# An encoder layer on one core: earlier first weights, and another order of loads at the weight switches and before the tail

## The chip, the cores and the metric

The kernel runs on one core of a Trainium2 chip. The metric is the time of one execution on the device in microseconds (us). The five engines that the profile names are PE (TensorE, matrix products), DVE (VectorE), ACT (ScalarE), POOL (GpSimd) and SP (SyncE, which here issues every DMA). Each engine works through its own instructions in order and waits where a semaphore tells it to.

## The reference

One layer of a bidirectional encoder is applied to two groups of 2048 tokens with a model width of 1024:

```python
h = rms_norm(x)
q_a, k_a, v_a, g_a, q_b, k_b, v_b, g_b = split(h @ w_in)      # 512,128,128,512, 512,512,512,512
o_a = windowed_gqa_sink(rope(norm(q_a)), rope(norm(k_a)), v_a) * silu(g_a)   # 8 heads, 2 kv heads, +-128 tokens
o_b = neighbourhood_attn(norm(q_b), norm(k_b), v_b, rpb) * silu(g_b)         # 8 heads, 8 x 16 window on a 64-wide grid
x = x + concat(o_a, o_b) @ w_out
return x + (p @ w_ple) * sigmoid(x @ w_ple_gate)
```

Branch A is a windowed attention with a sink, branch B a neighbourhood attention on a grid with a learned relative position bias. All is float32.

## The kernel before

**Precision.** Each float32 operand of a product is split into a high part and a low remainder, and a product is three matrix products. For weights `split_w` does it: ScalarE writes the high part (L147 with the norm's scale, L151 without), VectorE the low part (L148, L152). For a token tile `split` does it: ScalarE the high part (L294), GpSimd the low part (L295).

**Tiles.** Tokens go in tiles of 128, 16 per group, 32 in all. A running number f counts the work: f = 0 to 31 is branch A (`proj_a`, `unit_a`), f = 32 to 63 the first half of branch B's heads, f = 64 to 95 the second half (`proj_b`, `unit_b`). Then `out_ahead(0)` to `out_ahead(3)` compute the output projection (`pout`) of four blocks of 256 tokens each, in four products that are numbered mp 0 to 3. The rest of the output projection and the gate of the last line of the reference run in the tail, in a pool of their own ("c"), as products of seven on sums of blocks (`acca`, `accc`, operands `opd`, sums of weights `s1` to `s4`).

**Order.** The projections are generators, chained in `stream`. The attention units draw from the stream between their own steps, so that TensorE has projection work while a softmax runs. A unit of branch B follows its projection by six tiles: unit 57 runs beside the projection of tile 63, unit 89 beside that of tile 95. TensorE's instructions are pinned in program order (`pinned`). The other engines' are ordered by a scheduler from the program's order and its own estimates, save those that `P` (`tc.keep_in_program_order`) pins.

**The first two tiles** are projected together (`first`): `pk` (keys and values of branch A, weights `wx`), then `pq` (queries, weights `w_q`, tag "wa"), then `pg` (gates, `w_g`, tag "wb"). `load_first` stages two blocks of 128 rows of weights at a time in a buffer with the tag "p_t", of which there are three, and splits them at once. The keys and queries go through a normalisation on VectorE (a reciprocal root by iterations, L126 to L133; `kt` L413; `q` L454), a rotation on GpSimd (L426 to L429 for the keys), and a transpose on TensorE (`pkt`, `pqt`), which stands between the products of `pg`. PSUM comes from three pools: "pj" (three banks), "sc" (three) and "ms" (two). `pk`, `pq`, `pg` and `pout` take "pj"; the scores of the attention take "sc".

**Weight switches.** `paired` takes the last two tiles of each stage together (tiles 30 and 31, 62 and 63, 94 and 95), so that the first weight set ("wa") is free while both still use the second ("wb"). `load_w` issues eight loads of 256 KB and puts their splits in the list `jobs`, from which `pump` and `flush` take them while the next products run. "wa" is loaded after both tiles' first product (`pqk`), "wb" after the second tile is finished. At the same time SP issues what the units and tiles need: the tiles' inputs (`stx`, L277), the bias of a unit of branch B (L701), the values with their windows (`vw`, L705, read from `v_d`, where L662 stores `vb`), the unit's output (`ob_d`, L759), and weight rows for the sums (`raw`, L491). A bias has 288, 360, 384 or 512 columns for each of four heads; those of 512 are 1 MB, one for unit 57 and one for unit 89. The softmax (L217, VectorE) adds the bias to the scores (`scb`) in PSUM.

**Passage to the tail.** The sums `s2`, `s1`, `s3` are loaded first (twelve loads of 256 KB, L943), then the last block's inputs, then the raw inputs of the first tail group (`oar` L970 and `obr` L971, 1 MB each), then the residual's blocks. `out_ahead(3)` computes four `pout`. For each it loads a residual block `ev` (L835), adds it on VectorE (L836), which frees the PSUM bank, and stores it (L837). `prep(0)` and `prep(1)` make the first operands of the tail out of `oar` and `obr` (L1000, L1003).

Of the kernel before, what the change touches and what calls it, by code (L numbers as in the profile page):

```python
# [11 lines left out]
F32 = mybir.dt.float32  # L12
# [77 lines left out]
def emit(ctx, tc, io):  # L90
# [79 lines left out]

    def load_w(pool, tag, src, c0, nk, scaled):

        ws = []
        hold[0] = HOLD[tag[:2]]
        for j in range(nk):
            w = pool.tile([128, 2, 512], F32R, tag=f"{tag}{j}", name=f"{tag}{j}", bufs=1)
            raw = w[:, 1].bitcast(F32)
            nc.sync.dma_start(raw, src[128 * j:128 * j + 128, c0:c0 + 512])
            jobs.append((f"{tag}{j}", partial(split_w, w, raw, nw[:, j:j + 1] if scaled else None, P)))
            ws.append(w)  # L180
        return ws

    def load_first(j0, w, src):

        n = w[0].shape[-1]
        st = main.tile([128, 2, 512], F32, tag="p_t", name="ws", bufs=3)
        nc.sync.dma_start(st[:, :, :n], src.rearrange("(j p) c -> p j c", p=128))
        for i in range(2):
            split_w(w[i], st[:, i, :n], nw[:, j0 + i:j0 + i + 1])
# [79 lines left out]
    def load_block(key, tag, bufs):  # L269
        kind, f, i = key  # L270
        staged[key] = main.tile([128, 512], F32, tag=tag, name="st" + kind, bufs=bufs)
        if kind == "n":
            s, t = divmod(f, NT)
            src = io["x_n"][s][128 * t:128 * t + 128]
        else:
            src = io["x_a"][f] if f < 2 * NT else io["x_b"][f % (2 * NT)]
        nc.sync.dma_start(staged[key], src[:, 512 * i:512 * i + 512])  # L277
# [8 lines left out]
    def split(f, i, pin=lambda ins: ins):  # L286
# [30 lines left out]
    def big(shape, dt, name):  # L317
# [15 lines left out]
    for j in range(0, KT // 2, 2):  # L333
        load_first(j, w_q[j:j + 2], io["w_in"][128 * j:128 * j + 256, 256:768])
    for i in range(2):
        load_block(("n", 0, i), "s", SB)
# [24 lines left out]
    nc.sync.dma_start(mask, io["band"])  # L361
    ks_a = big([128, 2, SEQ], F32R, "ks_a")
# [28 lines left out]
    def proj_a(f):  # L391
# [4 lines left out]
        pk = ptile([128, 256], "pj", "pk")  # L396
# [130 lines left out]
    qrest = {}  # L527
# [83 lines left out]
    def proj_b(f):  # L611
# [47 lines left out]
        for w, (c0, ncol) in COL_WIN.items():  # L659
            lo, hi = max(c0, 16 * cb), min(c0 + ncol, 16 * cb + 16)  # L660
            if lo < hi:
                nc.sync.dma_start(v_d[half, s, w][8 * b:8 * b + 8, lo - c0:hi - c0].rearrange("r c h a d -> c r (h a d)"),  # L662
                                  v[8 * (lo - 16 * cb):8 * (hi - 16 * cb)].bitcast(F32).rearrange("p h a d -> p (h a d)"))
# [24 lines left out]
    def unit_b(f):  # L688
# [7 lines left out]
        if cb != 2:  # L696
            off, _ = BIAS_OFF[(row_type(b), col_type(cb))]
            if not bt:
                bt.append(big([128, 2, 4, 512], F32, "bias"))
            bt.append(bt[0][:, len(bt) % 2])  # L700
            nc.sync.dma_start(bt[-1][:, :, :n], io["bias"][half][:, off:off + 4 * n].rearrange("p (h n) -> p h n", h=4))  # L701
        bias = bt[-1]
        vw = [ap.tile([128, 4, 2 * HD], F32R, tag=("vp", "vr_")[j % 2], name="vw", bufs=3 - j % 2) for j in range(nch)]
        for j in range(nch):
            nc.sync.dma_start(vw[j][:kc].bitcast(F32).rearrange("p h d -> p (h d)"),  # L705
                              v_d[half, s, cb][r0 + rows * j:r0 + rows * j + rows]
                              .rearrange("r c h a d -> (r c) (h a d)"))
# [40 lines left out]
        def fin(_):  # L748
# [10 lines left out]
            nc.sync.dma_start(ob_d[s][b, :, 2 * half:2 * half + 2, cb, :], o_t)  # L759
# [17 lines left out]
    def load_o(n, tail):  # L777
        if n < len(tiles):
            s, u = tiles[n]
            o_st[n] = []  # L780
            for i in range(2):
                st = main.tile([128, 2, TW], F32, tag="stage", name="oa", bufs=2)
                nc.sync.dma_start(st, oa_d[s].rearrange("(i j p) t -> i p j t", p=128, j=2)[i, :, :, TW * u:TW * u + TW])
                o_st[n].append(st)
            for i in range(2):
# [4 lines left out]
                nc.sync.dma_start(st.rearrange("p j c t -> p (j c) t"),  # L790
# [25 lines left out]
    def out_ahead(n):  # L816
# [7 lines left out]
        for mp in range(4):  # L824
# [6 lines left out]
            if tail:  # L831
                ev = ap.tile([128, 2, TW], F32, tag="ev", name="ev", bufs=2)
            else:
                ev = main.tile([128, 2, TW], F32, tag="s", name="ev", bufs=SB)
            nc.sync.dma_start(ev, io["x_r"][n][:, 2 * mp:2 * mp + 2])  # L835
            nc.vector.tensor_tensor(out=ev, in0=ps, in1=ev, op=ALU.add)  # L836
# [34 lines left out]
    def paired(f, n):  # L871
# [53 lines left out]
    with tc.tile_pool(name="c", bufs=1) as op:  # L925
# [190 lines left out]
        prep(1)  # L1116
        ws[0]["s4"] = load_q(0, "s4")
# [106 lines left out]
```

## Time and profile before

| | before |
|---|---|
| median of 3 runs | 2605.88 us (2604.47 to 2607.68) |
| the profiled execution | 2603.58 us |
| span of its trace | 2601.7 us |
| mean granted TensorE clock | 0.994 |
| TensorE busy | 2547.1 us, 98% of the span |
| VectorE / ScalarE / GpSimd busy | 1963.3 / 1416.3 / 789.2 us |
| DMA | 357.51 MB, mean 137 GB/s |

The span is the time from the first to the last instruction on the core; the execution's own time is a little longer. In rows of the timeline a time is the start in us from the start of the span, the next number is the length, "x24" counts instructions that stand together, and a bracket gives the idle time before and what ended it. "out<-in" names the tiles that an instruction writes and reads. A row with SPq is the issue of a DMA, not its transfer. In rows of stretches each engine has its busy time in us with its count of instructions, then follow the granted clock, the share of time in which the DMA engines were busy, and the data rate in GB/s.

### The profile page before, as it was taken

The numbers are of one execution on the slowest core, as the hardware profiler recorded it, in microseconds if no ns is written. First come the engines' busy times: TensorE is split into PE (matmuls) and PEld (weight loads), VectorE is DVE, ScalarE is ACT, GpSimd is POOL, SyncE is SP. The second block draws the span as 40 slices with busy tenths as digits, with TensorE's granted clock in tenths as the row PEclk, the third lists the DMA queues.
The fourth block names the chain that finished last, engine by engine and source line by source line (L and its number), as shares of the span: only waits on it lengthen the run. The fifth ranks groups of instructions, "written<-read, shape, count | busy, mean of one in ns | idle before, by whom it ended". The sixth has DMA issues, their size and how long they took to land.

```text
span 2601.7 us, 47013 instructions
## 1 busy us (share of the span) xinstructions
PE 2547.1 (98%) x16080; PEld 2269.7 (87%) x16080; DVE 1963.3 (75%) x5702; ACT 1416.3 (54%) x3327; POOL 789.2 (30%) x996
## 2 busy tenths in 40 slices
PE   7999999999999999999999999999989999999999
PEld 6888888888877888888788888887989999999999
DVE  6888988889897788888888888888655648555454
ACT  5666666666675666666766666666432214222222
POOL 3333333333322333333233332321122423233321
PEclk9999999999999999999999999999999999999999
DMA  5333322111143564555654554457575445232221
GB/s 178 108 102 108 101 93 94 54 60 56 58 111 120 174 188 153 185 184 163 225 178 150 187 177 150 153 155 214 172 251 190 150 165 196 82 116 92 78 82 45
DMA packets 227519, 357.51 MB, mean 137 GB/s; under 512 B 37936, under 2 KB 115376, under 8 KB 222128
## 3 DMA queue, kind: packets, MB, share of 16 engines
q1 hardware_dynamic: 227280, 354.50, 42.8%
q8 instruction: 128, 2.10, 0.3%
q14 instruction: 111, 0.91, 0.1%
HBM read 266.33 MB, written 105.92 MB: 143 GB/s over the span
## 4 chain that ended last, share of the span: by engine, by line
PE 87%; DVE 5%; DMA 2%; ACT 2%; issue 2%; POOL 1%; SPq 0%; POOLq 0%; DVEq 0%; ACTq 0%
PE pqk L202 13%; PE pvg L202 12%; PE acca L1034 11%; PE accc L1034 9%; PE pg L202 6%; PE pq L202 5%; PE pob L202 4%; PE pple L202 3%; PE ptb L205 3%; PE scb L202 3%; PE pt L205 3%; PE po L202 3%; PE sc L202 3%; PE pk L202 3%; PE pout L202 3%
## 5 line engine op out<-in xcount | busy, mean ns | idle before, releaser
L232 ACT ACTIVATE s<-s,nm 128x384 f32<-128x384 f32 (+4 forms) x512 | 306.2, 599 | 340.6 <-DVE nm L228 185.0
L202 PE MATMUL pvg<-wb,xr 128*128 128x512 f32 x1536 | 455.2, 404 | 0.0
L202 PE MATMUL pqk<-wa,xr 128*128 128x512 f32 x1536 | 437.4, 407 | 0.0
L295 POOL TENSOR_TENSOR xr<-stx,xr 128x512 fp32r<-128x512 f32 x192 | 247.6, 1297 | 193.4 <-ACT xr L294 189.9
L202 PEld LDWEIGHTS pqk<-wa,xr 128*128 128x128 f32 x1536 | 267.5, 189 | 37.2
L202 PEld LDWEIGHTS pvg<-wb,xr 128*128 128x128 f32 x1536 | 267.4, 189 | 31.3
L202 PE MATMUL pg<-wb,xr 128*128 128x512 f32 x768 | 232.4, 410 | 4.1 <-DVE q L454 4.1
L202 PE MATMUL pq<-wa,xr 128*128 128x512 f32 x768 | 222.8, 404 | 3.6 <-ACT wa L147 2.8
L243 POOL TENSOR_TENSOR g<-qg,rd 128x256 f32<-128x256 f32 x64 | 39.7, 620 | 495.1 <-DVE rd L241 481.3
L1034 PE MATMUL acca<-opd,s 128*128 128x256 f32 x1344 | 164.6, 283 | 2.9 <-ACT r L1066 2.5
L1034 PEld LDWEIGHTS acca<-opd,s 128*128 128x128 f32 x1344 | 162.7, 192 | 3.6 <-ACT r L1066 2.7
L202 PEld LDWEIGHTS pq<-wa,xr 128*128 128x128 f32 x768 | 141.1, 191 | 28.3 <-ACT wa L147 3.4
L217 DVE CUSTOM_DVE_ANT_0 s<-scb,bias 128x288 f32<-128x288 f32 (+3 forms) x256 | 142.0, 555 | 29.1 <-PE scb L202 23.6
L202 PEld LDWEIGHTS pg<-wb,xr 128*128 128x128 f32 x768 | 137.9, 190 | 25.0 <-issue 4.6
L726 ACT CAST p_t<-ptb 96x384 fp32r<-96x384 f32 (+3 forms) x256 | 129.7, 508 | 54.1 <-PE ptb L205 52.3
L727 DVE TENSOR_TENSOR p_t<-ptb,p_t 96x384 fp32r<-96x384 f32 (+3 forms) x256 | 149.0, 584 | 9.1 <-ACT p_t L726 6.4
L607 ACT ACTIVATE ks_b<-pktb,wk 64x128 fp32r<-64x128 f32 x256 | 125.4, 490 | 49.1 <-DVE ks_b L608 40.6
L202 PEld LDWEIGHTS pob<-p_t,vw 128*128 128x128 f32 (+2 forms) x832 | 133.2, 190 | 20.8 <-DVE p_t L727 2.5
L608 DVE SCALAR_TENSOR_TENSOR ks_b<-pktb,wk,ks_b 64x128 fp32r<-64x128 f32 x256 | 115.1, 449 | 39.8 <-ACT ks_b L607 33.4
L202 PE MATMUL pob<-p_t,vw 128*128 128x256 f32 (+2 forms) x832 | 141.0, 283 | 2.0 <-DVE p_t L727 2.0
L1000 POOL TENSOR_TENSOR opd<-sum,opd 128x1024 fp32r<-128x1024 f32 x28 | 69.5, 2484 | 232.6 <-ACT opd L986 232.6
L217 DVE CUSTOM_DVE_ANT_0 s<-sc,mask 128x384 f32<-128x384 f32 (+1 forms) x256 | 135.8, 532 | 0.8
(197 smaller groups left out, 5909.1 us busy)
## 6 DMA issues: line engine op xcount, KB each, us to landing
stx<-x_b SPq DMA_DIRECT2D x128, 256.0 KB
vw<-v_d SPq DMA_DIRECT2D x112, 256.0 KB
stx<-x_a SPq DMA_DIRECT2D x64, 256.0 KB
stn<-x_n SPq DMA_DIRECT2D x64, 256.0 KB
v_d<-vb SPq DMA_DIRECT2D x64, 256.0 KB
x1r<-x_d SPq DMA_DIRECT2D x16, 1024.0 KB
y_t<-r SPq DMA_DIRECT2D x64, 256.0 KB
v_d<-vb SPq DMA_DIRECT2D x96, 128.0 KB
```

The costliest lines, as they stand in the source:

```text
L202: pinned(nc.tensor.matmul(out, lhsT, rhs, start=start, stop=stop))
L205: pinned(nc.tensor.transpose(out, in_, ident))
L217: nc.vector.tensor_tensor_reduce(out=s[:, :n], in0=ps[:, :n], in1=bias, scale=1.0, scalar=-3.0e38, op0=ALU.add, op1=ALU.max, accum_out=sm[ ...
L232: nc.scalar.activation(ss[i][:, :n], ss[i][:, :n], AF.Exp, bias=nm[:, i:i + 1], accum_out=den[:, i:i + 1])
L243: nc.gpsimd.tensor_tensor(out=g2, in0=gs.rearrange("p (h d) -> p h d", h=4), in1=rd.unsqueeze(2).broadcast_to([128, 4, HD]), op=ALU.mult)
L295: nc.gpsimd.tensor_tensor(out=lo, in0=raw, in1=hi.bitcast(F32), op=ALU.subtract)
L607: nc.scalar.activation(hi, pkt[a:a + 64, i], AF.Copy, scale=wk[a:a + 64, 1:2])
L608: nc.vector.scalar_tensor_tensor(out=lo, in0=pkt[a:a + 64, i], scalar=wk[a:a + 64, 1:2], in1=hi.bitcast(F32), op0=ALU.mult, op1=ALU.subtract)
L726: nc.scalar.copy(p_t[:kc, :nch, 0], pf)
L727: nc.vector.tensor_tensor(out=p_t[:kc, :nch, 1], in0=pf, in1=p_t[:kc, :nch, 0].bitcast(F32), op=ALU.subtract)
L1000: each(lambda x, y, z: eng.tensor_tensor(out=x, in0=y, in1=z, op=ALU.subtract), out, a, b)
L1034: pinned(nc.tensor.matmul(ps[:, kk], w[k][:, a, c:c + 128], o[:, b, k], start=i in (0, 1, 4) and kk == 0 and k == 0 and j == 0, stop=k == ...
```

## The change

Three places are edited.

1. **Start.** The first weights are loaded in one stream and split later. `wx` goes to two "p_t" buffers, the loads interleaved with those of the first token tile; `w_q` to "p_t" and a buffer "raw", `w_g` to "p_t" and "qg" buffers that are idle then. The low part of token tile 0 is made on VectorE instead of GpSimd. `pk` of the first two tiles takes a bank of "sc" instead of "pj".
2. **Weight switches.** The loads of `load_w` are pinned in program order, and after them the next 14 loads or stores that go through the new function `dma` (inputs, bias, `vw`, `v_d`, `ob_d`, `oa`, `ob`). The "wb" loads are moved into a hook, which the second tile calls right after its last products.
3. **Passage to the tail.** Three of the residual blocks of the last `out_ahead`, `oar`, `obr` and the fourth residual block are loaded first. The `s` loads follow after 24 products, their flush comes after `prep(1)`, and the adds of `ev` are pinned in program order.

```diff
+    held_loads = [0]
+
+    def dma(out, in_):
+        ins = nc.sync.dma_start(out, in_)
+        if held_loads[0] > 0:
+            held_loads[0] -= 1
+            P(ins)
...
     def load_w(pool, tag, src, c0, nk, scaled):
...
-            nc.sync.dma_start(raw, src[128 * j:128 * j + 128, c0:c0 + 512])
+            P(nc.sync.dma_start(raw, src[128 * j:128 * j + 128, c0:c0 + 512]))
...
+        held_loads[0] = 14
         return ws
 
-    def load_first(j0, w, src):
-
-        n = w[0].shape[-1]
-        st = main.tile([128, 2, 512], F32, tag="p_t", name="ws", bufs=3)
-        nc.sync.dma_start(st[:, :, :n], src.rearrange("(j p) c -> p j c", p=128))
-        for i in range(2):
-            split_w(w[i], st[:, i, :n], nw[:, j0 + i:j0 + i + 1])
+    def load_first(st, j, c, n):
+
+        k = st.shape[1]
+        nc.sync.dma_start(st[:, :, :n], io["w_in"][128 * j:128 * (j + k), c:c + n].rearrange("(j p) c -> p j c", p=128))
+        return [st[:, i, :n] for i in range(k)]
...
-        nc.gpsimd.tensor_tensor(out=lo, in0=raw, in1=hi.bitcast(F32), op=ALU.subtract)
+        low.tensor_tensor(out=lo, in0=raw, in1=hi.bitcast(F32), op=ALU.subtract)
...
+    st = [main.tile([128, 4, 256], F32, tag="p_t", name="ws", bufs=3) for _ in range(2)]
+    raws_x, raws_q, raws_g = [], [], []
     for i in range(2):
         load_block(("x", 0, i), "stage", 2)
+        raws_x += load_first(st[0][:, 2 * i:2 * i + 2], 2 * i, 0, 256)
     for i in range(2):
-        split(0, i)
-    for j in range(0, KT, 2):
-        load_first(j, [wx[:, j + i] for i in range(2)], io["w_in"][128 * j:128 * j + 256, 0:256])
+        raws_x += load_first(st[1][:, 2 * i:2 * i + 2], 4 + 2 * i, 0, 256)
     for i in range(2):
         load_block(("x", 1, i), "s", SB)
+    raws_q += load_first(main.tile([128, 2, 512], F32, tag="p_t", name="ws", bufs=3), 0, 256, 512)
+    raw = ap.tile([128, 4, 512], F32, tag="raw", name="ws", bufs=1)
+    for i in range(2):
+        raws_q += load_first(raw[:, 2 * i:2 * i + 2], 2 + 2 * i, 256, 512)
+    for i in range(2):
+        load_block(("n", 0, i), "s", SB)
+    for i in range(2):
+        split(0, i, low=nc.vector)
+        for j in range(2 * i, 2 * i + 2):
+            split_w(wx[:, j], raws_x[j], nw[:, j:j + 1])
+    for j in range(4, KT):
+        split_w(wx[:, j], raws_x[j], nw[:, j:j + 1])
     for i in range(2):
         split(1, i)
...
+    raws_q += load_first(main.tile([128, 2, 512], F32, tag="p_t", name="ws", bufs=3), 6, 256, 512)
+    for j in range(KT // 2):
+        split_w(w_q[j], raws_q[j], nw[:, j:j + 1])
...
+    for j in (0, 2):
+        raws_g += load_first(main.tile([128, 2, 512], F32, tag="p_t", name="ws", bufs=3), j, 768, 512)
+    for j in range(4, KT):
+        raws_g += load_first(ap.tile([128, 1, 512], F32, tag="qg", name="wg", bufs=6), j, 768, 512)
...
-        pk = ptile([128, 256], "pj", "pk")
+        pk = ptile([128, 256], "pj" if f > 1 else "sc", "pk")
...
     first = [filler(0), filler(1)]
-    for count, w, c in ((24, None, 0), (24, w_q, 256), (10 ** 9, w_g, 768)):
-        for j in range(KT // 2 if w is w_q else 0, KT if w else 0, 2):
-            load_first(j, w[j:j + 2], io["w_in"][128 * j:128 * j + 256, c:c + 512])
+    for count, w, raws in ((24, (), ()), (24, w_q, raws_q), (10 ** 9, w_g, raws_g)):
+        for j in range(KT // 2 if w is w_q else 0, len(w)):
+            split_w(w[j], raws[j], nw[:, j:j + 1])
...
+        hooks.pop(f, lambda: None)()
         v = ap.tile([128, 4, 2, HD], F32R, tag="sq", name="vb", bufs=2)
...
-            nc.sync.dma_start(bt[-1][:, :, :n], io["bias"][half][:, off:off + 4 * n].rearrange("p (h n) -> p h n", h=4))
+            dma(bt[-1][:, :, :n], io["bias"][half][:, off:off + 4 * n].rearrange("p (h n) -> p h n", h=4))
...
+        def second():
+            if half == 2:
+                split_o(0, 1)
+            w.append(load_w(main, "wb", src, c0 + 512, KT, half < 2))
+        hooks[f + 1] = second
         yield from b
-        if half == 2:
-            split_o(0, 1)
-        w.append(load_w(main, "wb", src, c0 + 512, KT, half < 2))
+        hooks.pop(f + 1, lambda: None)()
         w_b[half] = w
...
-            nc.sync.dma_start(ev, io["x_r"][n][:, 2 * mp:2 * mp + 2])
-            nc.vector.tensor_tensor(out=ev, in0=ps, in1=ev, op=ALU.add)
+            ev = evs[mp] if evs else load_ev(n, mp)
+            P(nc.vector.tensor_tensor(out=ev, in0=ps, in1=ev, op=ALU.add))
...
         ws = [{}, {}]
-        for name in ("s2", "s1", "s3"):
-            ws[0][name] = load_q(0, name)
         w_p = []
-        load_o(AHEAD - 1, False)
...
+        load_o(AHEAD - 1, False)
+        evs = [load_ev(AHEAD - 1, mp) for mp in range(3)]
         load_raw(0)
+        evs.append(load_ev(AHEAD - 1, 3))
+        LEAD = 2
+        ahead = out_ahead(AHEAD - 1, evs)
+        drain(ahead, 24)
+        for name in ("s2", "s1", "s3"):
+            ws[0][name] = load_q(0, name)
         for _ in range(3):
             load_x()
-        flush("0s3")
-        LEAD = 2
-        ahead = out_ahead(AHEAD - 1)
-        drain(ahead, 144)
+        drain(ahead, 120)
         prep(0)
         drain(ahead)
         w = w_b[2]
         ws[0].update(a11=w[0][:4], a12=w[0][4:], a22=w[1][4:])
         prep(1)
+        flush("0s3")
         ws[0]["s4"] = load_q(0, "s4")
```

The other loads that now go through `dma` (`stx`, `v_d`, `vw`, `ob_d`, `oa`, `ob`) change in no other way. `load_ev` is the load of `ev` that stood in `out_ahead` before. TensorE's instructions and their order are the same in both built programs.

More of the change, by code (lines that the diff above doesn't have):

```diff
@@ L276, in load_block @@
             src = io["x_a"][f] if f < 2 * NT else io["x_b"][f % (2 * NT)]
-        nc.sync.dma_start(staged[key], src[:, 512 * i:512 * i + 512])
+        dma(staged[key], src[:, 512 * i:512 * i + 512])
     def load_next():
@@ L284, in emit, with split @@
     xt, stats = {}, {}
-    def split(f, i, pin=lambda ins: ins):
+    def split(f, i, pin=lambda ins: ins, low=nc.gpsimd):
         if f >= 6 * NT:
@@ L525, in stats_b @@
         nc.vector.tensor_scalar_mul(hr_b[:, c], rs_b[:, c], 0.5)
-    qrest = {}
+    qrest, hooks = {}, {}
     def prep_a(f):
@@ L661, in proj_b @@
             if lo < hi:
-                nc.sync.dma_start(v_d[half, s, w][8 * b:8 * b + 8, lo - c0:hi - c0].rearrange("r c h a d -> c r (h a d)"),
+                dma(v_d[half, s, w][8 * b:8 * b + 8, lo - c0:hi - c0].rearrange("r c h a d -> c r (h a d)"),
                                   v[8 * (lo - 16 * cb):8 * (hi - 16 * cb)].bitcast(F32).rearrange("p h a d -> p (h a d)"))
@@ L704, in unit_b @@
         for j in range(nch):
-            nc.sync.dma_start(vw[j][:kc].bitcast(F32).rearrange("p h d -> p (h d)"),
+            dma(vw[j][:kc].bitcast(F32).rearrange("p h d -> p (h d)"),
                               v_d[half, s, cb][r0 + rows * j:r0 + rows * j + rows]
@@ L758, in fin @@
                                     in1=o_t.rearrange("p i (r c) -> p i r c", c=16), op=ALU.mult)
-            nc.sync.dma_start(ob_d[s][b, :, 2 * half:2 * half + 2, cb, :], o_t)
+            dma(ob_d[s][b, :, 2 * half:2 * half + 2, cb, :], o_t)
         return {"sc": sc, "pt": pt, "po": po, "fin": fin, "prep": lambda _: nxt(f)}
@@ L782, in load_o @@
                 st = main.tile([128, 2, TW], F32, tag="stage", name="oa", bufs=2)
-                nc.sync.dma_start(st, oa_d[s].rearrange("(i j p) t -> i p j t", p=128, j=2)[i, :, :, TW * u:TW * u + TW])
+                dma(st, oa_d[s].rearrange("(i j p) t -> i p j t", p=128, j=2)[i, :, :, TW * u:TW * u + TW])
                 o_st[n].append(st)
@@ L789, in load_o @@
                     st = main.tile([128, 2, 4, 64], F32, tag="s", name="ob", bufs=SB)
-                nc.sync.dma_start(st.rearrange("p j c t -> p (j c) t"),
+                dma(st.rearrange("p j c t -> p (j c) t"),
                                   ob_d[s][u // 2].rearrange("p (i j) c t -> i p (j c) t", i=2)
@@ L814, in o_hi_lo, with load_ev, out_ahead @@
         return lambda k, b: o_rs[n][k // 4][:, k % 4 // 2, b, k % 2, :]
-    def out_ahead(n):
+    def load_ev(n, mp):
+        if n < AHEAD - 1:
+            ev = ap.tile([128, 2, TW], F32, tag="ev", name="ev", bufs=2)
+        else:
+            ev = main.tile([128, 2, TW], F32, tag="s", name="ev", bufs=SB)
+        nc.sync.dma_start(ev, io["x_r"][n][:, 2 * mp:2 * mp + 2])
+        return ev
+    def out_ahead(n, evs=None):
         tail = n < AHEAD - 1
@@ L830, in out_ahead @@
                     yield c
[L831 to L834, printed above, removed]
-            nc.sync.dma_start(ev, io["x_r"][n][:, 2 * mp:2 * mp + 2])
-            nc.vector.tensor_tensor(out=ev, in0=ps, in1=ev, op=ALU.add)
+            ev = evs[mp] if evs else load_ev(n, mp)
+            P(nc.vector.tensor_tensor(out=ev, in0=ps, in1=ev, op=ALU.add))
             nc.sync.dma_start(x1_d[n][:, 2 * mp:2 * mp + 2], ev)
```

4 lines of the change are left out of this document (removed).

## The prediction, made before the changed kernel was run

> **What bounds the kernel now.** I read the page's totals first, then the split of the span into stretches, then the waits of TensorE.
>
> ```profile
> span 2601.7 us, 47013 instructions
> PE 2547.1 (98%) x16080; PEld 2269.7 (87%) x16080; DVE 1963.3 (75%) x5702; ACT 1416.3 (54%) x3327; POOL 789.2 (30%) x996
> ```
> ```profile
> 0.00:50.00 50.00, 34.75 (x140) 27.21 (x141) 29.79 (x104) 25.90 (x51) 16.05 (x33) 0.90 0.54 178
> 1250.00:1300.00 50.00, 44.35 (x226) 35.75 (x225) 44.92 (x112) 37.22 (x77) 15.36 (x16) 0.97 0.65 213
> 1750.00:1800.00 50.00, 45.06 (x245) 37.44 (x244) 43.45 (x129) 34.44 (x82) 9.87 (x14) 0.98 0.72 224
> 1900.00:1950.00 50.00, 43.16 (x335) 42.41 (x334) 30.40 (x43) 15.93 (x27) 13.54 (x12) 0.93 0.80 278
> ```
> ```profile
> PE pk L202 <- ACT wx L147: 7.2, 1, 7.2
> PE acca L1034 <- DVE ev L836: 5.3, 1, 5.3
> ```
>
> TensorE is busy for 2547.1 of 2601.7 us: 54.6 us are idle, and the diff changes neither its instructions nor their order. The stretches (length; busy time of PE, PE's weight load, DVE, ACT, POOL with counts; granted clock; DMA share; GB/s) show where the idle time lies: 15.25 us in the start, 5.65 at the switch into branch B's second half, 4.94 at the switch to the output weights, 6.84 in the passage to the tail. All four are places that the change touches. They hold 32.7 us; that, with some half-clock time, is all there is to win. What can be lost has no such limit, since TensorE stands in order behind whatever comes late. In the two switch stretches DVE is at 44.92 and 43.45 of 50, so it has little slack to make up a delay of its own.
>
> **The start.** TensorE's timeline (start, length, engine, line, operation, count, idle before and who ended it), then the stretches around its second stall, SP's and DVE's timeline, and POOL's rotation of the first keys:
>
> ```profile
> 22.82 0.79 PE L202 MATMUL pq<-wa,xr 128*128 128x512 f32 x1 [2.57 <-ACT wa L147]
> 24.17 10.79 PE L202 MATMUL pq<-wa,xr 128*128 128x512 f32 x35 [0.56 <-DVE wa L148]
> 39.01 1.30 PE L202 MATMUL pg<-wb,xr 128*128 128x512 f32 x4 [4.05 <-DVE q L454]
> ```
> ```profile
> 18.00:24.00 6.00, 3.04 (x11) 1.69 (x9) 4.79 (x17) 3.88 (x9) 0.00 (x0) 0.90 1.03 364
> 24.00:28.00 4.00, 3.83 (x9) 3.06 (x10) 3.83 (x16) 2.44 (x5) 0.34 (x1) 0.50 0.56 172
> ```
> ```profile
> 1.66 0.91 SPq L277 DMA_DIRECT2D stx<-x_a x2
> 2.60 1.46 SPq L187 DMA_DIRECT2D ws<-w_in  x3
> ```
> ```profile
> 33.20 0.75 DVE L148 SCALAR_TENSOR_TENSOR wb<-ws,nw,wb 128x512 fp32r<-128x512 f32 x1
> ```
> ```profile
> 34.01 0.75 DVE L148 SCALAR_TENSOR_TENSOR wb<-ws,nw,wb 128x512 fp32r<-128x512 f32 x1
> ```
> ```profile
> 27.66 0.81 POOL L426 TENSOR_TENSOR r<-kt,tab 128x32 f32<-128x32 f32 x1 [14.88 <-DVE kt L413]
> ```
> ```profile
> 28.92 0.25 POOL L429 TENSOR_TENSOR kt<-r 128x32 f32<-128x32 f32 x1
> ```
>
> Removed: (a) the first weights go out between the two halves of the first token tile, one issue (0.46 us, half of the 0.91) earlier and with 256 KB less ahead of them (0.7 us at 364 GB/s): about 1.1 us off the first wait of 7.2. (b) All of the query weights are on their way early instead of waiting for a staging buffer: the 2.57 and the 0.56 us go, and with them the 4 us at clock 0.50 behind (3.83 busy there is about 1.9 us of full-speed work): 5.0 together. (c) With the first keys' sums in another PSUM pool, the first gate product finds a free bank and needn't wait for q: 4.05. Together -10.2.
>
> Added: in the built order all eight gate-weight splits stand on DVE ahead of the first keys (kt), and on ScalarE the square of the second tile's queries stands ahead of six of them. The transpose of those keys is the eleventh TensorE instruction of the first gate product. So only when the second pq ends come six splits at 0.81 each (33.20 to 34.01), 4.9 us, with the square and what is left of the reciprocal root, some 2 by my estimate, and POOL's rotation, 1.5 (27.66 to 29.17): the keys are there 8.4 us after the end of pq. TensorE asks for them after ten products at that splitting pace or a little faster (35 in 10.79 above, half clock included), about 3 us after. So it waits some 5.4 us in a place that had no wait, with a little half clock behind: +6.2. Net **-4**; the bounds are -10.2 (keys in time) and +1 (the first queries late as well, by another rotation behind kt).
>
> **Switch 1** (branch A to B) has no bias and moves only SP's order by one store: 0, within 1 either way.
>
> **Switch 2** (tiles 62 and 63). What the first row below shows is the load of the 128x2048 bias, 1 MB, for unit 57, the first with 512-wide scores. It goes out 29 us ahead of its use (1258.74). After the change the fourteen next SP loads behind the "wa" weights are held in program order, and the built order is: eight wa, three v_d stores, two raw of 512 KB, this bias, four vw. The v_d stores wait for vb.
>
> ```profile
> 1229.62 0.36 SPq L701 DMA_DIRECT2D bias<-bias  x1
> ```
> ```profile
> 1258.34 0.48 DVE L657 SCALAR_TENSOR_TENSOR vb<-pvg,rs_b,vb 128x256 fp32r<-128x256 f32 x1
> 1258.74 0.68 DVE L217 CUSTOM_DVE_ANT_0 s<-scb,bias 128x512 f32<-128x512 f32 x1
> ```
> ```profile
> 1258.86 1.80 SPq L662 DMA_DIRECT2D v_d<-vb  x3
> 1260.70 0.95 SPq L491 DMA_DIRECT2D raw<-w_gate  x2
> 1261.75 1.28 SPq L705 DMA_DIRECT2D vw<-v_d  x2
> ```
> ```profile
> 1259.58 0.47 PE L202 MATMUL scb<-ks_b,q1b 128*128 128x512 f32 x1 [0.53 <-ACT qg L665]
> ```
> ```profile
> 1260.00:1264.00 4.00, 4.00 (x23) 3.28 (x22) 4.00 (x10) 3.95 (x8) 1.48 (x1) 1.00 0.85 242
> 1264.00:1269.00 5.00, 3.96 (x25) 2.98 (x23) 4.87 (x12) 4.30 (x12) 1.67 (x3) 1.00 0.95 356
> 1269.00:1280.00 11.00, 8.97 (x40) 7.27 (x39) 8.53 (x17) 8.56 (x18) 4.96 (x5) 0.84 0.67 207
> ```
>
> The softmax is the second DVE instruction behind vb (only qg stands between), so the bias is asked for just when it is needed. It goes out near 1261.7, where vw stands now, behind 0.5 MB of v_d and 1 MB of raw. Before, the DMA engines moved 0.97 MB in 1260 to 1264 and 1.78 MB in the five us after; the 2.5 MB are through near 1268.5. DVE stands with all its later work queued behind: weight splits, ks_b, p_t. TensorE has three score banks, so its fourth score product (1259.58) waits until about 1269.3: +9.7. Back come the waits that this stretch has now (5.00 less 3.96, and 11.00 less 8.97: 3.1), of which DVE, 4.87 of 5 busy, can give only some two: **+7.5**. From 4 (landing at 400 GB/s, all waits given back) to 11 (nothing given back, one more stretch of half clock).
>
> A rule to weigh here: the last of these rows grants 0.84 of the clock behind an idle of two us, and 24 to 28 grants 0.50 behind 2.57. The Trainium skill, "TensorE: Matmul & The Clock Gate", Part 1 (The HAM clock gate), says that the clock halves after an idle window of about 3.4 us and returns after as much busy time; this trace has it halved after less. By the page's window each new stall would cost an estimated 1.7 us more, and the sum would be some 3 us higher.
>
> The same notes' "DMA: Bandwidth & Descriptors" (Rules for kernel authors) asks to issue a transfer early and wait late, which speaks against this part. Its table has 1 MB in 6.15 us alone; by that the bias would land at 1267.9, and the sum be 0.6 lower.
>
> **Switch 3** (tiles 94 and 95) has the same bias for unit 89, and its softmax, but no raw:
>
> ```profile
> 1755.15 0.36 SPq L701 DMA_DIRECT2D bias<-bias  x1
> ```
> ```profile
> 1784.23 0.68 DVE L217 CUSTOM_DVE_ANT_0 s<-scb,bias 128x512 f32<-128x512 f32 x1
> ```
> ```profile
> 1784.34 1.84 SPq L662 DMA_DIRECT2D v_d<-vb  x3
> ```
>
> The bias goes out at 1786.2 with 0.5 MB ahead of it: 1.5 MB from about 1785.5 at 242 to 356 GB/s land between 1789.7 and 1791.7; I take 1790.5, +6.3 on 1784.23. Little comes back, DVE being the late one in this stretch: **+6.3**, from 3 to 9.
>
> **The passage to the tail.** TensorE's rows, then SP's, the chain's transfer, DVE's and POOL's.
>
> ```profile
> 1914.28 11.68 PE L202 MATMUL pout<-o_r,wb 128*128 128x256 f32 x96
> 1926.34 0.47 PE L1034 MATMUL acca<-opd,wa 128*128 128x256 f32 x2 [0.38 <-issue]
> 1927.56 2.89 PE L1034 MATMUL acca<-opd,wa 128*128 128x256 f32 x22 [0.74 <-DVE opd L1000]
> ```
> ```profile
> 1908.63 7.71 SPq L943 DMA_DIRECT2D s<-sums  x12
> ```
> ```profile
> 1917.34 10.31 DMA obr<-ob_d
> ```
> ```profile
> 1931.65 3.36 DVE L1003 TENSOR_TENSOR sum<-sum,oar 128x1024 f32<-128x1024 f32 x1
> 1934.93 1.28 DVE L836 TENSOR_TENSOR ev<-pout,ev 128x512 f32<-128x512 f32 x2
> ```
> ```profile
> 1928.07 3.37 POOL L1000 TENSOR_TENSOR sum<-obr,oar 128x256 f32<-128x256 f32 x4 [24.57 <-DMA ev<-x_r]
> ```
>
> Now obr goes out behind twelve loads of s, and ev of the last projection, which frees the PSUM bank for acca, stands on DVE behind a sum that needs it. Afterwards oar and obr go out ahead of those twelve (near 1908.6), obr lands near 1917, POOL's four sums end at 1920.4, DVE's sum at 1923.8, two splits later ev is done at 1925.7 instead of 1935.6. But the ev adds are held in order behind that sum, and this one frees the bank of the projection's fourth product, at which TensorE arrives near 1920.1 (half way through the 96): it waits 5.6 there in place of the 5.3 of acca and the 0.38 and 0.74. **-1**, from -6 (obr 5 us sooner) to +2 (obr as slow as now, 10.31, although less is ahead of it).
>
> **Sum** against the profiled execution (2603.58, span 2601.7): -4 + 0 + 7.5 + 6.3 - 1 = +8.8. The median shown, 2605.88, is 2.30 above that execution, so I forecast 2614.7 for the median.
>
> **Rivals.** *The other side, faster:* the bias does not gate. If the DMA engines serve it beside the v_d stores, or vb comes far enough ahead of the first softmax, it arrives with the scores. Then the switches cost nothing and give back some 3 us of the idle above: 2605.88 - 4 - 3 - 1 = 2597.9. Against it: 0.4 us between vb and softmax, and a transfer of 1 MB never under 2.5 us at the 400 GB/s that these stretches hardly reach. It decides from a landing within 1.5 us of vb. Chance 0.10. *The start and tail give all:* keys in time (-10.2) and ev early (-6), with the switches as forecast (+13.8), give 2603.5. For it: both waits that I add are worked out, not seen. Chance 0.15. *The switches cost more:* 11 and 9 with a half clock behind, and the start saves nothing: 2605.88 + 20 - 1 + 1 = 2626. For it: DVE at nine tenths has no room for a backlog of 16 us. Chance 0.15. *My forecast,* 2607 to 2622: 0.60.
>
> **How the numbers follow.** Two in ten lie outside 2603 to 2625: most of the first rival and a third of the third, and an edge of the second. About 0.2%, 5.2 us, is what a measurement of this kernel can tell from no change. Faster by more (under 2600.7): the first rival and a little of the second, 0.12. Within it: the rest of the second and the low end of my own, 0.20. Slower: 0.68.
>
> **What would show it.** In the trace after: DVE's 512-wide softmax near 1258 and 1784 waits for the DMA of its bias, some 9 and 6 us, with TensorE idle at the fourth score product; in the start the first pk near 6.1 us, no wait of pq near 20, and a wait of the first transposes for POOL's kt near 30 to 37; in the passage a wait of pout for DVE's ev near 1920 and none of acca. The forecast is wrong if the bias lands before vb, or if the transposes in the first gate product wait for nothing.

## The result and the profile after

The changed kernel takes 2624.45 us, the median of four runs (2622.44 to 2629.44), against 2605.61 us for the kernel before (2604.47 to 2607.68) on the same chip: a ratio of 1.0074, with an interval of 1.0057 to 1.0092. It is 18.8 us slower, where 8.8 had been forecast. The traced execution of after is the slowest of its four, 2629.44 us, so a second trace was taken of it later (2621.66 us) and both are used below.

The page's totals and the stretches around the edited places, after:

```profile
span 2626.2 us, 47007 instructions
PE 2554.0 (97%) x16080; PEld 2275.3 (87%) x16080; DVE 1963.5 (75%) x5704; ACT 1414.6 (54%) x3327; POOL 783.8 (30%) x994
```
```profile
0.00:50.00 50.00, 37.92 (x168) 30.84 (x169) 30.12 (x108) 27.05 (x55) 12.92 (x31) 0.93 0.54 190
1250.00:1300.00 50.00, 36.47 (x169) 29.45 (x168) 36.14 (x89) 28.45 (x57) 9.12 (x11) 0.83 0.59 199
1770.00:1820.00 50.00, 37.64 (x199) 31.04 (x197) 36.16 (x99) 29.29 (x68) 8.82 (x12) 0.90 0.54 171
```

TensorE's work is the same, 16080 instructions; in this trace its idle time has grown by 17.6 us, from 54.6 to 72.2, and its busy time by 6.9, from 2547.1 to 2554.0. The start got better (12.1 us idle for 15.25), and the two switches into units with 512-wide scores got worse: 13.5 us idle of 50 at the first and 12.4 at the second, with clocks of 0.83 and 0.90. (The second lies later than in before, so its window is 1770 to 1820.) What TensorE waits for, after (what waited, for whom: us in total, times, longest):

```profile
PE scb L209 <- DVE mx L224: 22.3, 3, 11.0
PE pout L209 <- DVE ev L865: 6.9, 1, 6.9
PE pk L209 <- ACT wx L147: 6.7, 1, 6.7
PE pout L209 <- DVE o_r L826: 5.0, 4, 1.8
PE pkt L212 <- POOL kt L452: 4.9, 2, 4.4
```

The first line was 1.0 us before and is now the largest wait. Who ends it is read from DVE, SP and TensorE at switch 2, in three timelines of after:

```profile
1258.97 0.48 DVE L681 SCALAR_TENSOR_TENSOR vb<-pvg,rs_b,vb 128x256 fp32r<-128x256 f32 x1
1260.22 0.42 DVE L690 SCALAR_TENSOR_TENSOR qg<-qg,pvg 128x256 f32<-128x256 f32 x1 [0.77 <-ACT qg L689]
1269.84 0.69 DVE L224 CUSTOM_DVE_ANT_0 s<-scb,bias 128x512 f32<-128x512 f32 x1 [9.20 <-DMA bias<-bias]
```
```profile
1259.49 2.09 SPq L174 DMA_DIRECT2D v_d<-vb  x3
1261.63 0.92 SPq L514 DMA_DIRECT2D raw<-w_gate  x2
1262.60 0.43 SPq L174 DMA_DIRECT2D bias<-bias  x1
```
```profile
1270.69 0.76 PE L209 MATMUL scb<-ks_b,q1b 128*128 128x512 f32 x1 [10.99 <-DVE mx L224]
1293.59 0.79 PE L209 MATMUL scb<-ks_b,q1b 128*128 128x512 f32 x1 [1.99 <-DVE mx L224]
1805.99 0.77 PE L209 MATMUL scb<-ks_b,q1b 128*128 128x512 f32 x1 [9.29 <-DVE mx L224]
```

It is a wait for a DMA, not for DVE. vb ends at 1259.45; only then can SP issue the three stores, then the two raws, then the bias at 1262.60. DVE does qg and sits idle for 9.20 us in front of the softmax. TensorE fills its three banks of scores and stops at the fourth product. The same chain at switch 3 ends in a wait of 9.29, with DVE idle for 7.73. The chain of work that ended last, followed back in after, has both transfers in it (start, length):

```profile
1262.60 7.11 DMA bias<-bias
...
1798.27 6.75 DMA bias<-bias
```

To split the loss by place, each TensorE instruction is compared with the same one in the trace of before (their order is the same): how much later it starts, in us. Columns are moments in the trace of before.

| kernel | 308 | 735 | 1197 | 1499 | 1900 | 2007 | 2587 |
|---|---|---|---|---|---|---|---|
| after, first trace | -4.3 | -2.9 | 0.6 | 12.1 | 22.2 | 23.2 | 24.6 |
| after, second trace | -5.0 | -4.3 | -2.6 | 9.0 | 19.7 | 18.3 | 18.3 |
| e1: only the loads late | 0.3 | 0.5 | 1.6 | 10.7 | 20.5 | 19.9 | 19.9 |
| e2: after, bias early | -4.5 | -4.5 | -2.9 | -3.0 | -1.1 | -2.7 | -2.8 |
| e3: start alone | -4.9 | -4.9 | -3.6 | -3.7 | -4.9 | -3.2 | -3.2 |
| e4: tail alone | -0.5 | -0.2 | 0.8 | -0.1 | 0.0 | -1.0 | -1.1 |
| e5: bias in four | -5.0 | -4.9 | -2.0 | 7.1 | 14.2 | 12.6 | 14.1 |
| e9: start, residual first | -3.5 | -3.0 | -1.8 | -1.9 | -1.7 | -5.5 | -4.3 |

By the two traces of after the start saves 4.3 to 5.0, switch 2 (1197 to 1499) costs 11.5 and 11.6, switch 3 (1499 to 1900) 10.1 to 10.7, and the passage (1900 to 2007) lies between -1.4 and +1.0. The two traces differ by 6 us at the end. Switches 2 and 3 have little part in it: it is 1.8 from the stretch of 735 to 1197, 3.8 from 1900 on, and 0.7 each from the start and the stretch behind it.

### The profile page after: what moved, and what is told of

Its sections match the earlier page's. It is cut to its first block, busy times and chain, and to the rows that moved or that the text cites. A ratio compares the mean times of both kernels' runs of the same rounds, so it can differ in the third digit from the quotient of the medians.

```text
span 2626.2 us, 47007 instructions
## 1 busy us (share of the span) xinstructions
PE 2554.0 (97%) x16080; PEld 2275.3 (87%) x16080; DVE 1963.5 (75%) x5704; ACT 1414.6 (54%) x3327; POOL 783.8 (30%) x994
## 4 chain that ended last, share of the span: by engine, by line
PE 86%; DVE 6%; DMA 3%; ACT 3%; issue 1%; POOL 0%; SPq 0%; DVEq 0%; ACTq 0%; POOLq 0%
PE pvg L209 12%; PE pqk L209 12%; PE acca L1064 12%; PE accc L1064 9%; PE pg L209 6%; PE pq L209 5%; PE pob L209 4%; PE pple L209 3%; PE scb L209 3%; PE pk L209 3%; PE ptb L212 3%; PE pt L212 3%; PE po L209 3%; PE sc L209 3%; PE pout L209 3%
## 5 line engine op out<-in xcount | busy, mean ns | idle before, releaser
L224 DVE CUSTOM_DVE_ANT_0 s<-scb,bias 128x288 f32<-128x288 f32 (+3 forms) x256 | 142.0, 555 | 48.0 <-PE scb L209 22.6
```

The lines of the kernel that those rows point to most:

```text
L224: nc.vector.tensor_tensor_reduce(out=s[:, :n], in0=ps[:, :n], in1=bias, scale=1.0, scalar=-3.0e38, op0=ALU.add, op1=ALU.max, accum_out=sm[ ...
```

## The experiments

Theory A is that of the prediction: a bias that goes out behind stores which wait for vb holds DVE, and by the score banks TensorE. Its rivals are named in what was expected.

**e1: before, with only those loads in the late order.** The stores of v_d of tiles 62 and 94 and the biases of units 57 and 89 are pinned in program order; nothing else changes.

```diff
-nc.sync.dma_start(v_d[...], ...)
+ins = nc.sync.dma_start(v_d[...], ...)
+if f in (62, 94):
+    P(ins)
...
+if f in (57, 89):
+    P(ins)          # the bias load
```

> The kernel before with one thing of the change alone: the v_d stores of tiles 62 and 94 and the 1 MB bias loads of units 57 and 89 are pinned in program order, so that these two biases go out behind the stores that wait for vb. Theory A (the two late biases are the whole cost of the switches): two waits of VectorE of 7 to 9 us for the bias, TensorE idle 9 to 11 us at the fourth score product of each, and 2605.6 + 20 = 2625 us (2621 to 2628). Rival B (the cost comes from the whole held order: vw and the next weights late as well): under +10, 2608 to 2615 us.

Measured: 2623.39 us against 2604.34, ratio 1.0068 (1.0054 to 1.0082), as theory A had it: the late loads alone cost 19.1 us, as much as the whole change. The waits of TensorE in e1, then DVE's row at switch 2:

```profile
PE scb L202 <- DVE mx L217: 22.6, 3, 11.2
PE pk L202 <- ACT wx L147: 7.4, 1, 7.4
PE acca L1038 <- DVE ev L840: 5.3, 1, 5.3
PE pg L202 <- DVE q L454: 4.2, 1, 4.2
```
```profile
1271.02 0.69 DVE L217 CUSTOM_DVE_ANT_0 s<-scb,bias 128x512 f32<-128x512 f32 x1 [9.38 <-DMA bias<-bias]
```

The scores wait as in after (22.6 for 22.3), while the waits of the start and the tail are those of before. The loss needs neither of the other two parts. By the table e1 costs 9.1 at switch 2, where after costs 11.5. The 2.4 between them are not a longer wait: from 1197 to 1499 TensorE's idle time grows by 9.3 us in e1 and 8.9 in after, but its busy time for the same instructions by 2.6 in after (1.6 in its second trace) and not at all in e1. That goes with the granted clock, which is 0.50 for 5.7 us after TensorE starts again in after and for 3.5 in e1; whether the held order has a part in it was not separated.

**e2: after, with the bias loads out of the held order.** The counter runs on, so all that stands behind them is held as in after. The edit frees every bias load, not only the two of 1 MB.

```diff
-dma(bt[-1][:, :, :n], ...)
+held_loads[0] -= held_loads[0] > 0
+nc.sync.dma_start(bt[-1][:, :, :n], ...)
```

> The changed kernel, with the bias loads alone taken out of the held order (they still count as one of the fourteen); everything else stays. Theory A: the two waits for the bias are gone, and the time is the start's gain, the tail's loss and nothing else: 2600 to 2606 us. Rival B: the held order of the other loads keeps at least half of the cost: over 2613 us.

Measured: 2601.5 us, ratio 0.9988 (0.9979 to 0.9996). With all the rest of the change in place the loss is gone and a small gain is left, as theory A had it. SP's and DVE's timeline in e2 at switch 2:

```profile
1226.77 0.36 SPq L726 DMA_DIRECT2D bias<-bias  x1
```
```profile
1255.88 0.68 DVE L224 CUSTOM_DVE_ANT_0 s<-scb,bias 128x512 f32<-128x512 f32 x1
```

The scheduler sends the bias 29 us ahead of its use, as in before, and the softmax has no bracket behind it: it waits for nothing. In the table e2 stays level from 1197 to 1499; from 1499 to 1900 it loses 1.9. Together e1 and e2 show the cause from both sides: the place of this one load in SP's queue at each of the two switches, and not the held order of the weight loads or the later "wb". What these cost is at most small: e2 is 2.2 us slower than e3, the start alone, and their intervals overlap.

**e5: after, with each of those biases as four loads of 256 KB, one for each head.** If the landing is what counts, the first softmax needs only the first quarter.

```diff
+if f in (57, 89):
+    for h in range(4):
+        dma(bt[-1][:, h, :n], io["bias"][half][:, off + n*h:off + n*h + n])
+    held_loads[0] += 3
...
```

> The changed kernel, with the 1 MB bias of units 57 and 89 loaded in four pieces of 256 KB, one per head, in the same place of the queue. Theory A (the queue is served in order, and the wait is 1 MB behind what was issued ahead): the first head's piece lands some 3 us sooner, TensorE's two waits at the fourth score product fall from 11.0 and 9.3 us to 6 to 8, and the time is 2617 us (2612 to 2620). Rival B (the pieces are served side by side, so that the first lands with the last): waits and time as they were, 2622 to 2627 us.

Measured: 2617.57 us, ratio 1.0049 (1.0035 to 1.0062), against 2605.62: +12.0 for after's +18.8. TensorE's timeline at the two switches in e5, then SP's issue and DVE's row at switch 3:

```profile
1266.51 0.77 PE L209 MATMUL scb<-ks_b,q1b 128*128 128x512 f32 x1 [9.50 <-DVE mx L224]
1798.08 0.76 PE L209 MATMUL scb<-ks_b,q1b 128*128 128x512 f32 x1 [6.38 <-DVE mx L224]
```
```profile
1793.60 1.95 SPq L174 DMA_DIRECT2D bias<-bias  x4
```
```profile
1797.24 0.69 DVE L224 CUSTOM_DVE_ANT_0 s<-scb,bias 128x512 f32<-128x512 f32 x1 [4.81 <-DMA bias<-bias]
```

The time is the forecast one. The waits shrink by 1.5 at switch 2, where 1 MB of raw still goes ahead, and by 2.9 at switch 3: 6.38 is in the range of 6 to 8 that was expected, 9.50 is not. Even the quarter comes 3.6 us after its issue at switch 3 (1793.60 to 1797.24). The rest of the wait is vb, the stores and that time; the earlier issue of e2 takes it away.

**e3 and e4: before, with the start alone and with the passage alone.** Their diffs are parts 1 and 3 of the change.

> The kernel before with the part on the first weights alone (early loads, first tiles' PSUM, low part of tile 0 on VectorE). My theory: third tile starts 4 to 5 us sooner, with a wait of about 4.4 us of the first key transpose for GpSimd's kt, and the whole is 2601.5 us (2600 to 2604). Rival: the gain of the start is given back before the tail, since the matched TensorE instruction was 4.3 us early at 300 us and 2.9 us early at 700 us: 2604 to 2607 us.

> The kernel before with the passage to the tail alone (residual blocks and raw inputs first, s loads after 24 products, adds of ev pinned). My theory: the wait of acca for ev (5.3 us) is replaced by one of pout for ev of 6 to 7 us, and the time is 2606.5 us (2605 to 2609). Rival: the long wait before the fourth pout costs a stretch of half clock in addition: 2609 to 2613 us.

Measured: e3 2599.32 us, ratio 0.9979 (0.9970 to 0.9988), a gain of 5.0; e4 2603.05 us, ratio 0.9998 (0.9989 to 1.0006), no difference that can be told. Both are a little better than their theories (2600 to 2604 and 2605 to 2609), and neither rival came. Waits of e3, then the one of the passage in e4:

```profile
PE pk L200 <- ACT wx L147: 6.5, 1, 6.5
...
PE pkt L203 <- POOL kt L443: 4.8, 2, 4.4
PE acca L1048 <- DVE ev L850: 4.1, 1, 4.1
```
```profile
PE pout L202 <- DVE ev L841: 6.1, 1, 6.1
```

The start trades its stalls for one of 4.4 at the first keys. The passage trades acca's wait of 5.3 for 6.1 of pout, for the same ev.

**e6 and e9: can the passage be made to pay?** Both have the start, and none of the switches. e6 has the tail part too, and keeps the splits of s out of the last projection until its fourth product. e9 keeps the tail of before and only orders the sum that needs obr behind the ev adds.

```diff
 # e6
-if i % 5 == 4:
+if i % 5 == 4 and (evs is None or mp > 2):
     pump()
 # e9
-nc.vector.tensor_tensor(out=ev, in0=ps, in1=ev, op=ALU.add)
+ev_made.append(nc.vector.tensor_tensor(out=ev, in0=ps, in1=ev, op=ALU.add))
...
+if n == 0:
+    tc.add_manual_dep(ins.ins, ev_made[-1].ins.name, ...)   # ins: the sum; order only
```

> The kernel before with the parts on the start and on the tail, without the weight switches' part, and the splits of s kept out of the last output projection until its fourth product, so that the first two adds of ev stand ahead of them on VectorE. Theory A (pout waited for ev because ev stood behind splits of late s loads): the wait of 6 to 7 us of pout is gone, acca waits under 2 us, 2593 us (2590 to 2596). Rival B: the wait passes on to the operands out of obr or to the late s: 2597 to 2601 us.

> The kernel before with the part on the start, and in the passage to the tail one order on VectorE alone: the first sum out of obr stands behind the adds of ev of the last output projection (loads and splits as in the kernel before). Theory A (in the kernel before, acca waited for ev only because ev stood behind that sum): the wait of 5.3 us falls under 2, and nothing else waits in its place, 2595 us (2593 to 2597). Rival B (the sum is needed as soon as ev, and accc or the second acca waits instead): 2598 to 2600 us, as the start alone.

Measured: e6 2596.67 us against 2605.62, ratio 0.9968 (0.9956 to 0.9981); e9 2597.86 against 2605.53, ratio 0.9967 (0.9955 to 0.9979). Both beat both kernels, and their intervals do not tell them apart. They do not tell either from the start alone, though (e3, 0.9970 to 0.9988), so that a gain in the passage is seen in the traces only: from 1900 to 2007 e9 gets 3.8 us ahead and e6 1.1, while e3 falls back by 1.7. Neither time reached its theory A (2593 and 2595 us). TensorE's waits at the passage, first e6, then e9:

```profile
PE acca L1050 <- DVE r L1077: 5.5, 2, 5.2
```
```profile
PE acca L1054 <- DVE ev L852: 2.4, 1, 2.4
...
PE acca L1054 <- DVE r L1081: 1.9, 2, 1.6
```

In e6 the wait for ev is gone, and the splits that were put off stand ahead of DVE's first result r: 5.2 us in another place. TensorE ran up to 13.7 us ahead of before and was 5.8 ahead at the end, as rival B had it. In e9 the residual's wait falls from 5.3 in before, or 4.1 in e3, to 2.4, where under 2 was expected; that is the smaller edit.

**e7 and e8: the first keys ahead of the gate splits.** e7 is e3 with VectorE's gate-weight splits from the fourth on ordered behind kt; e8 joins that and e6.

```diff
-split_w(w[j], raws[j], nw[:, j:j + 1])
+split_w(w[j], raws[j], nw[:, j:j + 1], *([behind_kt] if w is w_g and j > 2 else []))
```

> The kernel before with the part on the start alone, and the last five gate-weight splits of VectorE ordered behind the first keys kt. Theory A (the keys were late because eight splits stood ahead of them): the wait of pkt for GpSimd's kt falls from 4.4 us to under 1.5, and the time is 2596 us (2594 to 2598). Rival B: the gate product or the query transposes wait as long instead: 2598 to 2601 us.

> Both at once: start with the keys first, tail with ev first, weight switches as in the kernel before. If both theories hold and add up: 2590 us (2587 to 2594). If one of the two waits only moves: 2594 to 2598. If neither does anything: 2598 to 2602 us.

Measured: e7 2603.12 us, ratio 0.9993 (0.9984 to 1.0002); e8 2603.22, 0.9994 (0.9985 to 1.0003). Neither differs from before by its interval, both are slower than any forecast for them, and most of the start's gain is lost (in the trace of e7, 2.5 us ahead at 308 for the 4.9 of e3). TensorE's first transposes in e7, then POOL's timeline:

```profile
31.65 0.33 PE L203 MATMUL pkt<-ident,kt 128*128 128x128 f32 x1 [1.75 <-DVE vr L431]
31.73 5.26 PE L200 MATMUL pg<-wb,xr 128*128 128x512 f32 x14
42.54 1.12 PE L203 MATMUL pqt<-ident,q 128*128 128x128 f32 x4 [5.55 <-POOL q L453]
```
```profile
37.73 2.49 POOL L293 TENSOR_TENSOR xr<-stx,xr 128x512 fp32r<-128x512 f32 x2 [6.13 <-ACT xr L292]
40.17 0.26 POOL L450 TENSOR_TENSOR r<-kt,tab 128x32 f32<-128x32 f32 x1
```

The first transpose's wait is 2.6 us shorter (1.75, no longer for kt), but POOL now makes the low part of a later token tile and rotates the second keys before the first queries, and pqt waits 5.55. One stall had covered the next. e8 has that wait (5.6) and e6's (4.6), and no gain.

**e10: after once more.**

> The changed kernel once more, for a second trace. The waits are those of its first trace: 9 and 8 us of VectorE for the two biases, 4.4 us of pkt for kt, 5 to 7 us of pout for ev. The stretches of half clock that stand behind no long wait (near 758, 775 and 2236 us in the first trace) lie elsewhere or are missing, and the matched TensorE instruction at the end is 18 to 22 us late instead of 24.6.

Measured: 2621.66 us, with 23.8 us of scb's waits for mx (five, the longest 11.0), 5.7 for pout's ev and 4.4 for the first keys. The waits at the switches repeat; the 6 us less than in the first trace lie mostly elsewhere, 1.2 of them in pout's shorter wait. TensorE is 18.3 us late at the end, as expected. Of the three low-clock stretches two are gone (1.00 from 745 to 755 and from 2215 to 2235), but from 760 to 770 the clock is 0.83 again.

## Why the forecast came out as it did

The sign, the mechanism and every wait that the forecast named are there; the sizes of two terms, switches 2 and 3, are not. The sum was +8.8, and it measured +18.8, or +18.3 at the end of the second trace. 2624.45 lies above the 2607 to 2622 that the forecast called its own.

**Start (-4): right in its parts, and in its sum by some luck.** pq's 48 products run without a stall, pg's wait of 4.05 is gone, the first pk comes at 6.67 (forecast 6.1), and the keys wait 4.37 (forecast 5.4). TensorE's timeline of after:

```profile
6.67 9.63 PE L209 MATMUL pk<-wx,xr 128*128 128x256 f32 x48 [6.67 <-ACT wx L147]
16.14 11.30 PE L209 MATMUL pq<-wa,xr 128*128 128x512 f32 x48
35.03 0.48 PE L212 MATMUL pkt<-ident,kt 128*128 128x128 f32 x1 [4.37 <-POOL kt L452]
```

The traces give -4.3 and -5.0, e3 alone -5.0. Up to the keys TensorE is 11.7 and 12.7 us ahead, where 10.2 was forecast; from there on it loses 7.3, where 6.2 was. Both parts were 1 to 2.5 us too small, and the two errors largely cancel.

**Switch 1 (0): within the noise of the traces.** They show +3.5 and +1.7 between 735 and 1197, nearly all of it busy time (3.3 and 1.6), but e1 and e4, in which nothing changes there, have +1.1 and +1.0, and e3, which has only the start, +1.3.

**Switch 2 (+7.5): the wait right, what comes back wrong; it measured +11.5.** The fourth score product was to come 9.7 late and comes 10.5 late (10.99 of wait for the 0.53 that stood there before); DVE's wait was put at some 9 and is 9.20. Two us were to come back from waits that vanish. By the comparison of the same instructions, from this product to 1499, TensorE idles 3.55 us in after for 5.12 in before, so 1.6 come back, though a wait of 1.99 stands there at 1293.59. The clock, for which the sum had no term, takes more than that: the same products take 2.6 us longer. 10.5 - 1.6 + 2.6 = 11.5. In the second trace it is 10.5 - 0.5 + 1.6 = 11.6. The stretches of after:

```profile
1264.00:1270.00 6.00, 0.00 (x0) 0.00 (x0) 0.16 (x1) 0.00 (x0) 0.00 (x0) 0.50 0.99 386
1270.00:1278.00 8.00, 7.31 (x24) 5.97 (x25) 7.91 (x17) 4.57 (x11) 0.74 (x1) 0.60 0.44 141
1278.00:1290.00 12.00, 11.45 (x63) 9.27 (x62) 9.63 (x20) 10.52 (x22) 5.55 (x6) 1.00 0.74 242
```

While TensorE idles the clock falls to 0.50, and in the 8 us from 1270 it has a mean of 0.60. With 0.50 first and 1.00 behind, that is half clock for 6.4 us, to 1276.4: 5.7 of them after TensorE starts again at 1270.69, worth 2.9 us. From there TensorE is busy without a break (7.31 of the 8 us); it has no idle time from which to make up ground. Before has half clock of its own in this stretch (0.84 over 11 us), so the difference is less. The Trainium skill, "TensorE: Matmul & The Clock Gate", Part 1 (The HAM clock gate), names a busy window of about 3.4 us before full clock, an estimated 1.7 us for each stall. The trace has 2.9 behind this stall and 1.4 behind the one of switch 3, where half clock ends 2.9 us after TensorE starts again (1808.9). The sum by the page's window, some 3 us higher, lay nearer than mine.

**Switch 3 (+6.3): the transfer mis-sized; it measured +10.1 to +10.7.** The bias goes out when it was to (1798.27 is 1786.2 and the 12.1 us that TensorE is late by then), but it was taken to land 4.3 us after its issue, and lands after 6.75. The 2.45 us between them take the term from 6.3 to 8.8, and 8.8 is by how much TensorE's 9.29 exceeds the 0.48 that stood there before. This is the step that failed. After's stretch from issue to landing:

```profile
1798.27:1805.02 6.75, 0.00 (x0) 0.00 (x0) 0.00 (x0) 0.24 (x1) 0.00 (x0) 0.53 0.88 300
```

The rate is within the 242 to 356 GB/s that were taken; the bytes are not the 1.5 MB that were added up. In the 6.75 us the DMA engines moved 2.0 MB: nearly all of v_d's 0.5, the bias, and most of the two loads of vw of 256 KB each that go out right behind it. A sum of the bytes ahead of a load leaves out those behind it. That they slow it was not tried alone, but in e1 loads also follow, from 1799.82 on, and DVE gets its bias 7.9 us after the issue (1796.92 to 1804.78). What is left of the term, 1.3 and 1.7 us, is 0.9 and 1.4 of waits behind the stall and 0.3 to 0.4 of busy time; e2 loses 1.9 in this stretch with its bias early, so that part needn't be the bias's. Low clock adds little here, because before has half clock at the same place (0.50 from 1797.8 to 1808.0). The upper bound of the term was 9.

**Passage (-1): right in mechanism; its size is within the noise.** e4 gives -1.0 in its trace, by 0.3 more idle time and 1.3 less busy time, and the two traces of after give +1.0 and -1.4. So the agreement in size is luck. DVE's timeline of after, then TensorE's:

```profile
1944.58 3.36 DVE L1033 TENSOR_TENSOR sum<-sum,oar 128x1024 f32<-128x1024 f32 x1 [3.48 <-POOL sum L1030]
1947.86 1.28 DVE L152 TENSOR_TENSOR s<-s 128x512 fp32r<-128x512 f32 x2
1949.06 0.68 DVE L865 TENSOR_TENSOR ev<-pout,ev 128x512 f32<-128x512 f32 x1
```
```profile
1949.79 8.58 PE L209 MATMUL pout<-o_r,wb 128*128 128x256 f32 x48 [6.87 <-DVE ev L865]
1958.21 5.92 PE L1064 MATMUL acca<-opd,wa 128*128 128x256 f32 x48
```

The sum, two splits, then ev: the order is the foretold one, pout waits (6.87 for 5.6) half way through its 96 products, and acca waits for nothing.

**The rivals.** That the bias does not gate is refuted by e1, and e2, where it is made true, comes to 2601.5: the 3 us that this rival counted as given back at the switches did not come. The rival nearest to the result is the third, switches of 11 and 9 (measured 11.5 and 10.1 to 10.7); but its other half, that the start saves nothing, is wrong, so its 2626 agrees with the median only in part by the mechanism it named. The second, start and tail giving all, is refuted by the waits that were worked out and came, 4.37 for the keys and 6.87 for ev. The rule of the Trainium skill that was weighed at switch 2, "DMA: Bandwidth & Descriptors", Rules for kernel authors (issue early, wait late), is what e2 and after measure: -2.8 us against before with a load of 1 MB at each of two switches issued 29 us early, +18.8 with both behind three stores.

## What to carry to other kernels

A queue that issues in order makes every load behind a waiting store as late as that store's source: before pinning an order of loads, look up for each when its consumer asks for it and what the queue ahead of it waits for. Size a late transfer by the bytes of its neighbours on both sides, or by the measured time of one that has such neighbours, and price each stall of TensorE with the low clock behind it, less what the stretch has already. Where a stall is removed, name what is late next and move that in the same edit: e6 and e7 only moved the wait; e9 moved one instruction and left 2.4 of 5.3 us.

## What was not expected of the hardware

Runs of after spread by 7 us, from 2622.4 to 2629.4. Part of that shows in stretches far from any edit. Near 763 us TensorE waits for 1.2 and then for 0.9 us in the traces of before and of after alike; before keeps the full clock and after is granted 0.50 for 3.41 us. Two neighbouring stretches of 3.41 us in before, then in after:

```profile
760.78:764.19 3.41, 2.19 (x10) 1.38 (x8) 3.41 (x6) 3.36 (x7) 0.00 (x0) 1.00 0.02 5
764.19:767.60 3.41, 2.59 (x12) 2.23 (x13) 3.41 (x15) 0.71 (x1) 0.61 (x1) 1.00 0.01 2
```
```profile
761.00:764.41 3.41, 1.34 (x6) 0.82 (x6) 3.41 (x9) 2.89 (x5) 0.61 (x1) 1.00 0.00 0
764.41:767.82 3.41, 3.41 (x10) 2.73 (x9) 3.38 (x17) 0.00 (x0) 0.00 (x0) 0.50 0.01 2
```

The clocks of all twelve traces say what decides it here. Between 15 and 2590 us every stretch of half clock in them lasts one to four steps of 3.41 us, and within one trace all of them lie on one grid of such steps; where the grid lies differs from trace to trace. There are 72 falls from full to half clock. A step at full clock in which TensorE was busy for less than 0.46 of the time was followed by one at half clock without exception, one with more than 0.51 never; between the two it went either way. Full clock came back after a step of half clock with more than 0.85 busy always, with less than 0.82 never. In after both waits fall into one step (1.34 of 3.41 is 0.39); in before the grid parts them (0.64 and 0.76). So the same waits cost clock or not by where they fall on the grid. These runs were made for other questions; no run moved a wait on the grid on purpose.
